# A hybrid decoder block on one core: quarter-array products of a recurrence issued in turns

## The chip, the core and the metric

The kernel runs on one core of one Trainium2 chip. TensorE multiplies matrices in a 128x128 array: a product takes a stationary operand (weights, loaded first) and streams a moving operand through it; results go to PSUM, in which this kernel keeps eight tiles of 128 partitions by 512 fp32 columns. A product whose contraction uses 64 partitions and whose output has 64 partitions occupies one quarter of the array: the half of the rows in which its operands lie, and the half of the columns that belongs to the partitions of its output. The profile prints such a product as 64*64. VectorE (DVE), ScalarE (ACT) and GpSimd (POOL) work elementwise and move PSUM results to SBUF; SyncE (SP) issues most loads from memory. [...]

The metric is the device time of one execution in microseconds (us), the median of several runs. Lower is better.

## The reference

One trunk layer on 512 tokens of 1024 channels: a norm, one wide projection, a sparse attention mixer (compressed, selected and window branches), an RWKV-7 mixer, two gates, an output projection with residual, then a gated MLP with a short convolution. Cut to the parts that the change touches:

```python
def compress_blocks(kv, pe, w1, w2):          # blocks of 32 tokens, stride 16 -> 31 compressed keys or values
    ...
    return jax.nn.gelu(flat @ w1) @ w2        # w2 is the second layer, 256 -> 64

def step(state, inp):                         # RWKV-7: 8 heads, state 64x64 per head, 512 tokens
    r_t, w_t, k_t, v_t, a_t, b_t = inp
    sa = jnp.einsum('bhij,bhj->bhi', state, a_t)
    state = state * w_t[:, :, None, :] + sa[..., None] * b_t[:, :, None, :] + v_t[..., None] * k_t[:, :, None, :]
    return state, jnp.einsum('bhij,bhj->bhi', state, r_t)
_, y = lax.scan(step, state0, xs)             # then a norm per head, a bonus term and a gate
```

## The kernel before

The dense projections keep fp32 accuracy with split operands: activations and weights are cut into a high and a low part, and three products (high x high, low x high, high x low) are summed. Weights arrive as `raw` tiles through SP (three buffers); ACT writes the high part `whi` and DVE or, for a few tiles, POOL the low part `wlo` (two buffers each, line 306).

The recurrence (lines 976 to 1032) is computed in eight chunks of 64 tokens. Products of the eight heads are laid out in four pairs `p` of two heads `r`; head `r` lives on partitions 64r to 64r+63. For chunk `c`, in the order in which TensorE gets it:

1. products from the carried state `M0` into `X` (operand `AR[...,0]`) and then into the output `Y` (operand `AR[...,1]`), 8 products each; both write partitions 64r, so both use the same two quarters. In the profile they are `ps_b<-M,AR` and `ps_a<-M,AR`.
2. DVE copies `X` to `Xs`; meanwhile TensorE runs a piece of other work ("fill").
3. 8 products of the inverse with `Xs` into `U` (`ps_b<-Xs,AB`), then 8 products `x_own` that begin the next chunk's `X` (`ps_b<-UV,AB`). The first use the quarters (rows r, columns r), the second (rows 1-r, columns r).
4. ACT and DVE copy `U` into `UV`; a piece of fill runs meanwhile.
5. 8 products for the next state (`ps_a<-UV,BKT`), which DVE turns into `M`, and 8 more that complete `Y` (`ps_a<-UV,AB`); ACT copies `Y` to `Ys`. Another piece of fill follows.

The fill is a generator, `fill_chain` (line 922): the rest of the keys' and values' projection, `compress`, and the gates' projections. In this stage TensorE's order is written by hand (`manual_schedule` with TensorE alone); the other engines' order comes from a scheduler.

`compress` (line 828) ends with the second layer: a group of 4 small products for the keys and 4 pairs for the values, and after each pair of the values an ACT copy into `vcb`, all from one PSUM bank `kc_ps`.

Ahead of the recurrence, the triangular inverses are put together from 32x32 blocks (`below`, `left`, lines 782 to 800): two visits of `below`, two of `left`, with pieces of a projection of width 280 (`kv_proj(1, 280)`) between them. That projection has three weight tiles; POOL writes all three low parts, and the third takes the buffer of the first.

Of the kernel before, what the change touches and what calls it, by code (L numbers as in the profile page):

```python
# [23 lines left out]
DH = 64  # L24
H = 8
NH2 = H // 2
C = 64
NCH = S // C
# [55 lines left out]
def hybrid_block(ctx: ExitStack, tc: tile.TileContext, A: dict, out: bass.AP):  # L84
# [34 lines left out]
    def pb():  # L119
        return bank("b", 2)  # L120

    def mm(o, l, r, start, stop):
        te.matmul(o, lhsT=l, rhs=r, start=start, stop=stop)  # L123

    def act(o, i, f=AF.Copy, **kw):
        sc.activation(o, i, f, **kw)  # L126
# [278 lines left out]
    def run(g):  # L405
        while True:
            try:
                next(g)
            except StopIteration as e:
                return e.value  # L410
# [23 lines left out]
    AR = mp.tile([128, NH2, NCH, 2, C], F32, name="AR", tag="AR")  # L434

    AB = abp.tile([128, NCH, NH2, 2, 128], F32, name="AB")
    BKT = rp.tile([128, NCH, NH2, 2, DH], F32, name="BKT")
    UV = rp.tile([128, NCH, NH2, 2, DH], F32, name="UV")
# [227 lines left out]
    for g in range(2):  # L666
        for b in range(2):
            r = 64 * g + 32 * b
# [107 lines left out]
    for b in (1, 0):  # L776
        for g in range(2):
            r = 64 * g + 32 * b
# [14 lines left out]
    def left(q0):  # L793
        ptr = [pa(), pb()]
        for i in range(16):
            for g in range(2):
                mm(ptr[g][half(g, 0), 32 * i:32 * i + 32], Y1[half(g, 1), q0 + i], ABq[g][half(g, 1), q0 + i, 32:64],
                   True, True)
        for g in range(2):
            act(ABq[g][half(g, 0), q0:q0 + 16, 32:64], ptr[g][half(g, 0)].rearrange("p (q t) -> p q t", t=32))  # L800
# [3 lines left out]
    with tc.manual_schedule(engines={mybir.EngineType.PE, mybir.EngineType.Pool}):  # L804
        for m in range(NGA):
            act(siga[m], dense_fm(hh, hl))
        below(0)
        below(16)
        next(fill)
        left(0)  # L810
        next(fill)
        left(16)
        next(fill)
        norm_keys(0)
        rstd(qss.rearrange("p t h -> p (t h)"), DH)
        for t in range(NT):
            nc.gpsimd.tensor_tensor(heads(qn[:, t]), heads(qn[:, t]), qss[:, t, :, None].to_broadcast([128, 8, DH]),
                                    op=ALU.mult)
# [11 lines left out]
    def compress():  # L830
        Rk = [sg1[:, 2 * a:2 * a + 2].rearrange("p m s -> p (m s)").rearrange("p (j g n) -> p j g n", j=16, g=2)
              for a in range(2)]
        for a, s_ in enumerate("kv"):
            v.memset(Rk[a][:, :, :, 31:32], 0.0)
            r0 = ROWS["cmp_pe_" + s_][0]
            for g in range(2):
                dv = Dc[:, a, g].rearrange("p (n j) -> p j n", j=8)
                for jh in range(2):
                    tt(Rk[a][:, 8 * jh:8 * jh + 8, g, 0:31], dv[:, :, jh:31 + jh],
                       prm[:, r0 + 8 * jh:r0 + 8 * jh + 8, None].to_broadcast([128, 8, 31]), ALU.add)  # L840
        cw2, hid, hidT, kcd = (QK[:, o:o + 256] for o in range(3072, 4096, 256))
        cw2 = cw2.rearrange("p (a m d) -> p a m d", a=2, m=2)
        hidT = hidT.rearrange("p (m a n) -> p m a n", m=2, a=2)
        kcd = kcd[0:32].rearrange("p (g a d) -> p g a d", g=2, a=2)
        kcs = cp.tile([32, 2], F32, name="kcs")
        yield
        hx = mmb()[:, 0:256]
        for s4 in range(4):
            w = [wnext(4, 256) for _ in range(2)]
            for j in range(4):  # L850
                for a in range(2):
                    mm(hx[64 * a:64 * a + 64], Rk[a][:, 4 * s4 + j].rearrange("p g n -> p (g n)"), w[a][:, j],
                       s4 + j == 0, s4 + j == 6)
            if s4 == 1:
                for a, s_ in enumerate("kv"):
                    nc.sync.dma_start(cw2[:, a], A["cmp_w2_" + s_][0].rearrange("(m p) d -> p m d", p=128))
            yield
        act(hid, hx, AF.Square)
        ts(hid, hid, 0.044715, 1.0)
        tt(hid, hid, hx, ALU.mult)  # L860
        act(hid, hid, AF.Tanh, scale=math.sqrt(2.0 / math.pi))
        stt(hid, hid, 1.0, hx, ALU.add, ALU.mult)
        yield
        pt = mmb()
        for m in range(2):
            te.transpose(pt[:, 128 * m:128 * m + 128], hid[:, 128 * m:128 * m + 128], ident)
        act(hidT.rearrange("p m a n -> p (m a n)"), pt[:, 0:256])
        yield
        kc_ps = mmb()
        for g in range(2):  # L870
            for m in range(2):
                mm(kc_ps[0:32, 64 * g:64 * g + 64], hidT[:, m, 0, 32 * g:32 * g + 32], cw2[:, 0, m], m == 0, m == 1)
        nc.gpsimd.memset(vcb, 0.0)
        for g in range(2):
            for e in range(2):
                bs = slice(64 * g + 32 * e, 64 * g + 32 * e + 32)
                for m in range(2):
                    mm(kc_ps[bs, 128:192], hidT[:, m, 1, 32 * g:32 * g + 32], cw2[:, 1, m], m == 0, m == 1)
                act(vcb[bs, 2 * g + e], kc_ps[bs, 128:192], AF.Copy, scale=0.5)
        for g in range(2):  # L880
            act(kcd[:, g, 0], kc_ps[0:32, 64 * g:64 * g + 64], AF.Copy, scale=0.5)
            act(kcd[:, g, 1], kcd[:, g, 0], AF.Square, accum_out=kcs[:, g:g + 1])
        rstd(kcs, DH)
        for g in range(2):
            ts(kcd[:, g, 1], kcd[:, g, 0], kcs[:, g:g + 1], None)
            ts(kcd[:, g, 0], kcd[:, g, 0], kcs[:, g:g + 1], None)
        yield
        pt = mmb()
        for g in range(2):
            te.transpose(pt[:, 32 * g:32 * g + 32], kcd[:, g].rearrange("p a d -> p (a d)"), ident[0:32, 0:32])  # L890
        ptv = pt[:, 0:64].rearrange("p (g n) -> p g n", g=2)
        act(KC[:, :, 0], ptv, AF.Copy, scale=kg)
        stt(KC[:, :, 1], ptv, kg, KC[:, :, 0].bitcast(F32), ALU.mult, ALU.subtract)

    def group_norm(c0, Ys):
# [6 lines left out]
        act(sq, Ys, AF.Square)  # L902
        v.tensor_reduce(n1, sq, axis=AX.X, op=ALU.add)
        rstd(n1, DH, 64e-5, "g")
# [55 lines left out]
    def hsl(r, n=64):  # L960
        return slice(64 * r, 64 * r + n)

    def x_own(c, X):
        for p in range(NH2):
            for r in range(2):
                o = hsl(1 - r)
                mm(X[hsl(r), 64 * p:64 * p + 64], AB[o, c, p, r, 0:64], UV[o, c, p, r, :], p == 0,
                   c == 0 and p == NH2 - 1)


    with tc.manual_schedule(engines={mybir.EngineType.PE}):
        M0 = Ys = gn = None
        X = pb()
        x_own(0, X)
        next(fill, None)
        for c in range(NCH):
            Y = pa()
            if M0 is not None:
                for p in range(NH2):
                    for r in range(2):  # L980
                        mm(X[hsl(r), 64 * p:64 * p + 64], AR[hsl(r), p, c, 0, :], M0[hsl(r), p, :], False,
                           p == NH2 - 1)
                for p in range(NH2):
                    for r in range(2):
                        mm(Y[hsl(r), 64 * p:64 * p + 64], AR[hsl(r), p, c, 1, :], M0[hsl(r), p, :], p == 0, False)
            Xs = tp.tile([128, NH2, DH], F32, name="Xs", tag="Xs", bufs=2)
            v.tensor_copy(Xs, X[:, 0:256].rearrange("p (a d) -> p a d", d=DH))
            next(fill, None)
            U = pb()
            for p in range(NH2):  # L990
                for r in range(2):
                    mm(U[hsl(r), 64 * p:64 * p + 64], AB[hsl(r), c, p, r, 0:64], Xs[hsl(r), p], True, True)
            act(UV[0:64, c, :, 0, :], U[0:64, 0:256].rearrange("p (a d) -> p a d", d=DH))
            v.tensor_copy(UV[64:128, c, :, 1, :], U[64:128, 0:256].rearrange("p (a d) -> p a d", d=DH))
            if c < NCH - 1:
                X = pb()
                x_own(c + 1, X)
            next(fill, None)
            if c < NCH - 1:
                Mp = pa()  # L1000
# [10 lines left out]
                    tt(M1, M1, pc, ALU.mult)  # L1011
            for p in range(NH2):
                for r in range(2):
                    mm(Y[hsl(r), 64 * p:64 * p + 64], AB[:, c, p, r, 64:128], UV[:, c, p, r, :],
                       M0 is None and p == 0, p == NH2 - 1)
            if c % 2 == 0:
                Ys = tp.tile([128, H, DH], F32, name="Ys", tag="Ys", bufs=2)
            for r in range(2):
                act(Ys[hsl(c % 2), r::2, :], Y[hsl(r), 0:256].rearrange("p (h d) -> p h d", d=DH))
            if c % 2 == 1:  # L1020
                gn = group_norm(c - 1, Ys)
                if c < NCH - 1:
# [1 line left out]
            M0 = M1  # L1024
# [306 lines left out]
    with tc.manual_schedule(engines=KTS):  # L1331
        for t in range(NT):
            qs = slice(128 * t, 128 * t + 128)
            p = mmb()
# [66 lines left out]
    for f in range(NF):  # L1401
# [4 lines left out]
        g = f // 2  # L1406
# [222 lines left out]
```

## Time and profile before

| | |
|---|---|
| median of 3 runs | 834.87 us (834.24 to 835.76) |
| profiled execution | 834.91 us, its span 833.1 us |
| TensorE busy | 812.8 us, 98% of the span |
| DVE, ACT, POOL busy | 604.0, 440.7, 70.5 us |
| stretch 165 to 290 us (inverses' end, recurrence) | TensorE busy 123.97 of 125.00 us |
| granted TensorE clock | full in every slice |

The span is what lies between the first and the last instruction; 1.8 us of the profiled execution lie outside it. A row of the timeline gives the start, the time until the last of its instructions ends, the engine, the line, what is written from what, the shape and the count. A product of fp32 operands stands as two instructions, one for each pass, so that 8 products are a row of x16. Line 123 is the helper through which all products go, so the tiles' names tell them apart. A busy TensorE is a sequence of overlapping instructions: a start-to-start distance says more than a duration.

### The profile page before, as it was taken

To read this page: it belongs to the slowest core of one execution; us is meant where nothing else is said; L and a number is where in the kernel's file an instruction comes from. 1 tells how busy PE (TensorE), PEld (TensorE's weight loads), DVE (VectorE), ACT (ScalarE), POOL (GpSimd) and SP (SyncE) were. 2 spreads that over 40 slices of the span, in tenths; PEclk is the share of its full clock that TensorE was granted. 3 is DMA by queue.
4 is the path that set the end of the run, shared out by engine and by line. 5 is a ranking of instruction groups with operands and counts; after the bars stand their busy time and mean duration, and the time that the engine had idled before them with its cause. 6 is when DMAs were issued, how large, how long until landed. Compare 5 with 4: busy or idle time off the path is not lost.

```text
span 833.1 us, 13078 instructions
## 1 busy us (share of the span) xinstructions
PE 812.8 (98%) x5039; PEld 663.3 (80%) x5039; DVE 604.0 (72%) x1154; ACT 440.7 (53%) x847; POOL 70.5 (8%) x92
## 2 busy tenths in 40 slices
PE   7999999999999999999999999999999999999997
PEld 5788878897778886787788888888888888877886
DVE  5678889963655578888585467667666677769997
ACT  6777755452545677776444354444444444453452
POOL 5200020140000020011000000000000000002101
PEclk9999999999999999999999999999999999999999
DMA  7432322335452230000147143333333332375753
GB/s 217 117 101 71 82 64 77 93 105 159 127 114 65 64 89 13 14 27 26 51 161 254 40 154 99 101 101 100 90 91 100 101 101 86 122 272 183 231 190 142
DMA packets 111394, 91.59 MB, mean 110 GB/s; under 512 B 4237, under 2 KB 98116, under 8 KB 111204
## 3 DMA queue, kind: packets, MB, share of 16 engines
q1 hardware_dynamic: 106192, 75.34, 30.9%
q0 software_dynamic: 4080, 12.87, 4.9%
q10 hardware_dynamic: 1060, 2.55, 1.0%
q8 instruction: 39, 0.64, 0.3%
q14 instruction: 23, 0.19, 0.1%
HBM read 85.30 MB, written 4.39 MB: 108 GB/s over the span
## 4 chain that ended last, share of the span: by engine, by line
PE 49%; DVE 2%; ACT 1%; DMA 1%; issue 0%; DVEq 0%; ACTq 0%
PE ps_mm L123 42%; PE ps_b L123 3%; PE ps_a L123 3%; DMA raw<-in_w_down_dram 1%; DVE wlo L306 1%; ACT whi L126 1%; DVE hl L138 0%; DVE raw L129 0%; DVE a L129 0%; DVE x1b L1437 0%; PE ps_b L1227 0%; ACT a L126 0%; PE ps_a L203 0%; PE ps_mm L1227 0%; ACT hh L126 0%
## 5 line engine op out<-in xcount | busy, mean ns | idle before, releaser
L123 PE MATMUL ps_mm<-hh,whi 128*128 128x512 f32 (+1 forms) x624 | 242.5, 390 | 0.4 <-ACT hh L126 0.3
L123 PE MATMUL ps_mm<-hl,whi 128*128 128x512 f32 (+1 forms) x624 | 238.9, 385 | 0.3 <-DVE hl L138 0.2
L306 DVE TENSOR_TENSOR wlo<-raw,whi 128x1024 fp32r<-128x1024 f32 (+1 forms) x107 | 125.5, 1174 | 95.8 <-PE ps_mm L123 74.4
L126 ACT ACTIVATE whi<-raw 128x1024 fp32r<-128x1024 f32 (+2 forms) x130 | 128.3, 988 | 100.9 <-PE ps_mm L123 42.5
L123 PE MATMUL ps_mm<-hh,wlo 128*128 128x512 f32 (+1 forms) x624 | 151.8, 384 | 0.0
L123 PEld LDWEIGHTS ps_mm<-hh,whi 128*128 128x128 f32 x624 | 117.2, 188 | 26.0 <-issue 1.1
L123 PEld LDWEIGHTS ps_mm<-hl,whi 128*128 128x128 f32 x624 | 117.3, 188 | 23.4 <-DVE hl L138 1.0
L123 PEld LDWEIGHTS ps_mm<-hh,wlo 128*128 128x128 f32 x624 | 115.1, 188 | 23.4
L138 DVE SCALAR_TENSOR_TENSOR cgq<-ps_mm,cw,cgq 128x511 f32<-128x511 f32 (+1 forms) x88 | 65.4, 746 | 1.6
L126 ACT ACTIVATE cgq<-ps_mm,cw 128x512 f32<-128x512 f32 x44 | 34.4, 781 | 19.5 <-PE ps_mm L123 18.9
L126 ACT ACTIVATE P<-P,nm 128x512 f32<-128x512 f32 (+3 forms) x64 | 35.4, 553 | 14.9 <-DVE nm L1201 14.9
L126 ACT ACTIVATE a<-cgq 128x512 fp32r<-128x512 f32 (+2 forms) x24 | 13.2, 549 | 54.1 <-DVE cgq L129 54.1
L129 DVE TENSOR_TENSOR cgq<-cgq 128x512 f32<-128x512 f32 (+1 forms) x52 | 36.4, 700 | 3.6 <-DMA cgq<-in_w_down_dram 1.9
L126 ACT ACTIVATE cgq<-cgq 128x512 f32<-128x512 f32 x22 | 13.9, 632 | 45.0 <-DVE cgq L138 45.0
L306 POOL TENSOR_TENSOR wlo<-raw,whi 128x512 fp32r<-128x512 f32 (+3 forms) x13 | 20.4, 1572 | 146.3 <-PE ps_mm L123 57.3
L1201 DVE CUSTOM_DVE_ANT_0 P<-ps_a,AB 128x512 f32<-128x512 f32 (+3 forms) x64 | 29.4, 483 | 4.2 <-PE ps_a L123 3.7
L1460 POOL DMA_DIRECT2D cgq<-in_w_down_dram x12 | 6.4, 535 | 296.6 <-DVE cgq L129 246.7
L126 ACT ACTIVATE ring<-cgq 128x1024 fp32r<-128x1024 f32 x12 | 12.7, 1062 | 19.4 <-PE ps_b L123 12.1
L123 PE MATMUL ps_a<-KH,qst 128*128 128x512 f32 (+3 forms) x64 | 21.3, 348 | 1.6 <-DVE nm L1201 0.9
L123 PE MATMUL ps_mm<-whi,hh 128*128 128x280 f32 (+2 forms) x72 | 22.4, 333 | 0.4 <-DVE AB L129 0.4
L126 ACT ACTIVATE QK<-ps_mm 128x64 f32<-128x64 f32 (+5 forms) x56 | 14.8, 307 | 14.4 <-PE ps_mm L123 14.3
L123 PE MATMUL ps_mm<-whi,hl 128*128 128x280 f32 (+2 forms) x72 | 21.7, 323 | 0.0
(427 smaller groups left out, 1486.1 us busy)
## 6 DMA issues: line engine op xcount, KB each, us to landing
raw<-in_w_up_dram SPq DMA_DIRECT2D x44, 512.0 KB, 3.8
raw<-in_w_in_dram SPq DMA_DIRECT2D x38, 512.0 KB, 3.9
raw<-in_w_down_dram SPq DMA_DIRECT2D x25, 512.0 KB, 4.5
cgq<-in_w_down_dram POOLq DMA_DIRECT2D x12, 512.0 KB, 4.6
raw<-in_w_out_dram SPq DMA_DIRECT2D x8, 512.0 KB, 3.6
xt<-in_x_dram SPq DMA_DIRECT2D x4, 512.0 KB, 5.8
raw<-in_cmp_w_k_dram SPq DMA_DIRECT2D x4, 512.0 KB, 4.2
raw<-in_cmp_w_v_dram SPq DMA_DIRECT2D x4, 512.0 KB, 4.8
```

The source lines that it names most:

```text
L123: te.matmul(o, lhsT=l, rhs=r, start=start, stop=stop)
L126: sc.activation(o, i, f, **kw)
L129: v.tensor_tensor(o, a, b, op=op)
L138: v.scalar_tensor_tensor(o, a, s, b, op0=op0, op1=op1)
L306: eng.tensor_tensor(lo, raw, hi.bitcast(F32), op=ALU.subtract)
L1201: v.tensor_tensor_reduce(out=P[:, i], in0=sp[:, N * (i - i0):N * (i - i0) + N], in1=BT[:, h, 384 - 128 * qt:512], scale=-1.0, scalar=-NEG, ...
L1460: nc.gpsimd.dma_start(raws[g][i], A["w_down"][0][256 * g + 128 * i:256 * g + 128 * i + 128])
```

## The change

- In step 1, the products into `X` and into `Y` are issued in turns, one of each. The `Y` products now write the partitions of the other head (`hsl(1 - r)`), so they use the quarters (rows r, columns 1-r), which `X` does not use. The products that complete `Y` and the copies to `Ys` are exchanged in the same way.
- In step 3, the products into `U` and the `x_own` products of the next chunk are issued in turns. The copies of `U` stand behind both.
- In `compress`, all products of the second layer come first and the four ACT copies behind them.
- `left(16)` follows `left(0)` directly; the piece of fill that stood between them comes after.

```diff
@@ the inverses @@
         left(0)
+        left(16)
         next(fill)
-        left(16)
         next(fill)
@@ compress @@
                     mm(kc_ps[bs, 128:192], hidT[:, m, 1, 32 * g:32 * g + 32], cw2[:, 1, m], m == 0, m == 1)
+        for g in range(2):
+            for e in range(2):
+                bs = slice(64 * g + 32 * e, 64 * g + 32 * e + 32)
                 act(vcb[bs, 2 * g + e], kc_ps[bs, 128:192], AF.Copy, scale=0.5)
@@ the recurrence @@
+    def in_turns(*gens):
+        gens = list(gens)
+        while gens:
+            for g in list(gens):
+                if next(g, gens) is gens:
+                    gens.remove(g)
+
+    def from_state(c, a, B, off, start, stop):
+        for p in range(NH2):
+            for r in range(2):
+                mm(B[hsl(1 - r if off else r), 64 * p:64 * p + 64], AR[hsl(r), p, c, a, :], M0[hsl(r), p, :],
+                   start and p == 0, stop and p == NH2 - 1)
+                yield
+
+    def through(c, U, Xs):
+        for p in range(NH2):
+            for r in range(2):
+                mm(U[hsl(r), 64 * p:64 * p + 64], AB[hsl(r), c, p, r, 0:64], Xs[hsl(r), p], True, True)
+                yield
...
-                for p in range(NH2):
-                    for r in range(2):
-                        mm(X[hsl(r), 64 * p:64 * p + 64], AR[hsl(r), p, c, 0, :], M0[hsl(r), p, :], False,
-                           p == NH2 - 1)
-                for p in range(NH2):
-                    for r in range(2):
-                        mm(Y[hsl(r), 64 * p:64 * p + 64], AR[hsl(r), p, c, 1, :], M0[hsl(r), p, :], p == 0, False)
+                in_turns(from_state(c, 0, X, False, False, True), from_state(c, 1, Y, True, True, False))
...
-            for p in range(NH2):
-                for r in range(2):
-                    mm(U[hsl(r), 64 * p:64 * p + 64], AB[hsl(r), c, p, r, 0:64], Xs[hsl(r), p], True, True)
+            if c < NCH - 1:
+                X = pb()
+                in_turns(through(c, U, Xs), x_own(c + 1, X))
+            else:
+                run(through(c, U, Xs))
             act(UV[0:64, c, :, 0, :], U[0:64, 0:256].rearrange("p (a d) -> p a d", d=DH))
             v.tensor_copy(UV[64:128, c, :, 1, :], U[64:128, 0:256].rearrange("p (a d) -> p a d", d=DH))
-            if c < NCH - 1:
-                X = pb()
-                x_own(c + 1, X)
...
-                    mm(Y[hsl(r), 64 * p:64 * p + 64], AB[:, c, p, r, 64:128], UV[:, c, p, r, :],
+                    mm(Y[hsl(1 - r), 64 * p:64 * p + 64], AB[:, c, p, r, 64:128], UV[:, c, p, r, :],
...
-                act(Ys[hsl(c % 2), r::2, :], Y[hsl(r), 0:256].rearrange("p (h d) -> p h d", d=DH))
+                act(Ys[hsl(c % 2), r::2, :], Y[hsl(1 - r), 0:256].rearrange("p (h d) -> p h d", d=DH))
```

How TensorE's order changes is shown at three places.

TensorE, recurrence, chunk 1, the products from the state (`M` is the carried state, `AR` the rows of `X` and `Y`, `ps_b` is `X`, `ps_a` is `Y`); before:

```order
L123 MATMUL ps_mm<-hl,whi 128x512
L123 MATMUL ps_b<-M,AR 64x64 [waits DVE_49]
L123 MATMUL ps_b<-M,AR 64x64 x7
L123 MATMUL ps_a<-M,AR 64x64 [waits PE_49]
L123 MATMUL ps_a<-M,AR 64x64 x7
L123 MATMUL ps_mm<-hh,whi 128x512
```

and now:

```order
L123 MATMUL ps_mm<-hl,whi 128x512
L123 MATMUL ps_b<-M,AR 64x64 [waits DVE_49]
L123 MATMUL ps_a<-M,AR 64x64 [waits PE_49]
L123 MATMUL ps_b<-M,AR 64x64
L123 MATMUL ps_a<-M,AR 64x64
...
L123 MATMUL ps_mm<-hh,whi 128x512
```

The 16 products are the same; `Y`'s first has moved from the ninth place to the second, with its wait. The products of `U` and `x_own` are mixed in the same way.

TensorE, second layer of the compression (`QK` holds its operands), chunk 4; before:

```order
L123 MATMUL ps_mm<-QK 32x64 [waits Activation_49]
L123 MATMUL ps_mm<-QK 32x64 x5
L123 MATMUL ps_mm<-QK 32x64 [waits Activation_49]
L123 MATMUL ps_mm<-QK 32x64
...
L123 MATMUL ps_mm<-hh,whi 128x512
```

and now:

```order
L123 MATMUL ps_mm<-QK 32x64 [waits Activation_49]
L123 MATMUL ps_mm<-QK 32x64 x11
L123 MATMUL ps_mm<-hh,whi 128x512
L123 MATMUL ps_mm<-hl,whi 128x512
L123 MATMUL ps_mm<-hh,whi 128x512
```

Three waits for ACT have gone from between the products.

TensorE, the second visit of `left` (`AB` holds the blocks, `sg` the inverses), a piece of the difference. The `wlo` rows between are the fill's 12 products with the first tile's low part:

```order
+L123 MATMUL ps_a<-AB,sg_1239 32x32
+L123 MATMUL ps_b<-AB,sg_1239 32x32
 L123 MATMUL ps_mm<-wlo,hh 128x280 x12
-L123 MATMUL ps_a<-AB,sg_1239 32x32
-L123 MATMUL ps_b<-AB,sg_1239 32x32
 L123 MATMUL ps_mm<-whi,hh 128x280
 L123 MATMUL ps_mm<-whi,hl 128x280
```

The 32 small products (two of them shown) stood between the 12 products with `wlo` and the next 10 with `whi`; now these follow each other.

More of the change, by code (lines that the diff above doesn't have):

```diff
@@ L968, in x_own @@
                    c == 0 and p == NH2 - 1)
+                yield
[15 more added lines that the diff above has]
+                mm(U[hsl(r), 64 * p:64 * p + 64], AB[hsl(r), c, p, r, 0:64], Xs[hsl(r), p], True, True)
+                yield
     with tc.manual_schedule(engines={mybir.EngineType.PE}):
@@ L973, in hybrid_block @@
         X = pb()
-        x_own(0, X)
+        run(x_own(0, X))
         next(fill, None)
```

## The prediction

> **What bounds the kernel now.** I read the page first, then a view of the stage by windows, then who waits for whom there, then the timeline of TensorE around each edit.
>
> ```profile
> PE 812.8 (98%) x5039; PEld 663.3 (80%) x5039; DVE 604.0 (72%) x1154; ACT 440.7 (53%) x847; POOL 70.5 (8%) x92
> PEclk9999999999999999999999999999999999999999
> 165.00:290.00 125.00, 123.97 (x1486) 99.98 (x1484) 69.34 (x171) 60.84 (x135) 11.59 (x15) 1.00 0.42 107
> 290.00:410.00 120.00, 116.71 (x771) 91.31 (x770) 95.42 (x309) 83.83 (x217) 14.30 (x16) 1.00 0.14 36
> PE ps_mm L123 <- ACT kc L126: 0.9, 3, 0.3
> DVE Xs L987 <- PE ps_b L123: 12.5, 4, 4.0
> DVE M L129 <- PE ps_a L123: 11.1, 4, 3.4
> ```
>
> The first two rows are from the page, the next two are stretches by windows (length, then busy time of PE, PEld, DVE, ACT, POOL), and the last three are waits around this stage (us, count, the longest). From 165 to 290 us TensorE is busy for 123.97 of 125 us at the full clock, and the only wait that the trace names for it is 0.9 us, for the ACT copies of the compression. DVE waits for TensorE, not the reverse. So TensorE's own time is the path here, and a microsecond that its instructions need less should reach the end; all four edits lie in this stretch. From 290 to 410 us it is idle for 120 - 116.71 = 3.3 us, in chains with ACT and DVE that begin from its own products and so move with it as a whole.
>
> **The recurrence's products.** The timeline of TensorE in chunk 1 (start, us until the last ends, what, count of passes):
>
> ```profile
> 193.84 0.68 PE L123 MATMUL ps_b<-M,AR 64*64 64x64 f32 x16
> 194.36 0.63 PE L123 MATMUL ps_a<-M,AR 64*64 64x64 f32 x16
> 194.92 0.50 PE L123 MATMUL ps_mm<-hh,whi 128*128 128x512 f32 x1
> ...
> 197.87 0.51 PE L123 MATMUL ps_b<-Xs,AB 64*64 64x64 f32 x10
> 198.16 0.27 PE L123 MATMUL ps_b<-UV,AB 64*64 64x64 f32 x2
> 198.21 0.28 PE L123 MATMUL ps_b<-Xs,AB 64*64 64x64 f32 x3
> 198.27 0.22 PE L123 MATMUL ps_b<-UV,AB 64*64 64x64 f32 x1
> 198.28 0.22 PE L123 MATMUL ps_b<-Xs,AB 64*64 64x64 f32 x1
> 198.28 0.22 PE L123 MATMUL ps_b<-UV,AB 64*64 64x64 f32 x1
> 198.33 0.22 PE L123 MATMUL ps_b<-Xs,AB 64*64 64x64 f32 x1
> 198.33 0.22 PE L123 MATMUL ps_b<-UV,AB 64*64 64x64 f32 x1
> 198.33 0.22 PE L123 MATMUL ps_b<-Xs,AB 64*64 64x64 f32 x1
> 198.34 0.51 PE L123 MATMUL ps_b<-UV,AB 64*64 64x64 f32 x11
> 198.78 0.44 PE L123 MATMUL ps_mm<-raw,sg 128*64 128x256 f32 x2
> ```
>
> The two groups from the state take 194.92 - 193.84 = 1.08 us, one after the other, on the same two quarters. `U` and `x_own` take 198.78 - 197.87 = 0.91 us for as many passes, and the rows say why: they lie on different quarters, and for a moment all four run. From 198.21 to 198.34, 0.13 us, eight passes start, four of `Xs` and four of `UV`, two per quarter: a quarter starts a pass every 0.06 us. In the last row `UV` is alone on two quarters: the 11th pass ends at 198.85 and takes 0.22, so it started at 198.63, ten starts after 198.34, five per quarter: 0.29 / 5 = 0.058. A quarter keeps its pace whether two run or four. That is the row that carries the forecast: what `in_turns` makes the rule has happened by chance here for a tenth of a microsecond.
>
> A group of 16 products now gives each quarter 8 passes. The first row of `Xs` has ten starts, five per quarter, the last at 197.87 + 0.51 - 0.22 = 198.16, so four distances of a quarter fill 0.29 us; at 0.058 for three of them the first is 0.11. From the last start to the first of other work it is 198.78 - 198.63 = 0.15. So 0.11 + 6 x 0.058 + 0.15, with 0.02 for four quarters begun one behind the other: 0.63 us. If the first loads of four quarters get in each other's way, as they never do in this trace, I allow 0.70. From below, no less than this is to be had while a quarter needs 0.058.
>
> From the state, chunks 1 to 7: 7 x (1.08 - 0.63) = 3.15 us less. `U` with `x_own`, chunks 0 to 6: 0.28 each. `X` and `U` are complete no later than before, since each needs the same 0.46 us from its first start to its last; but what came behind them on TensorE, and covered the copies, is gone. One place has no cover to give:
>
> ```profile
> 217.40 1.07 PE L123 MATMUL ps_a<-UV,BKT 128*64 128x64 f32 x15
> ...
> 246.12 0.69 PE L123 MATMUL ps_a<-UV,BKT 128*64 128x64 f32 x16
> ...
> 214.68 1.06 ACT L126 ACTIVATE whi<-raw 128x1024 fp32r<-128x1024 f32 x1 [3.13 <-DMA raw<-in_w_in_dram]
> ...
> 215.77 1.23 DVE L306 TENSOR_TENSOR wlo<-raw,whi 128x1024 fp32r<-128x1024 f32 x1 [0.89 <-ACT whi L126]
> 217.36 0.43 DVE L994 COPY UV<-ps_b 64x256 f32<-64x256 f32 x1
> ```
>
> In chunk 2 the state's products need 1.07 us against 0.69 for 16 passes in chunk 4, since DVE's `UV` copy ends only at 217.79; it stands behind a `wlo`, which waited for `whi`, which waited for a load. ACT had been idle for that load since 211.55, before `U` began, so the copy does not come sooner for a shorter `U`: chunk 2 gives its 0.28 back as a longer wait. Six chunks are left: 6 x 0.28 = 1.7 us; with chunk 2, 2.0 at most. The tightest of the others is chunk 4, where the chain of the compression stands ahead of the copy:
>
> ```profile
> 240.51 0.16 DVE L135 TENSOR_SCALAR rs_m<-kcs 32x2 f32<-32x2 f32 x1 [1.00 <-ACT QK L126]
> ...
> 243.78 0.43 DVE L994 COPY UV<-ps_b 64x256 f32<-64x256 f32 x1
> ```
>
> There 246.12 - 244.21 = 1.9 us lie between copy and use. The edit in the compression takes 1.8 of them from TensorE's side and `U` 0.28, but DVE's chain, which today waits 1.00 us for ACT, begins about 1 us sooner too. I expect no wait; 0.5 us if I am wrong. The exchanged heads move nothing between engines. Where the products into the state end on one pair of columns and those into `Y` now begin on the same, a quarter may wait a pass or two, up to 0.05 in each of 8 chunks; I take 0.1 together, 0 to 0.4.
>
> **The compression's second layer.**
>
> ```profile
> 236.38 0.86 PE L123 MATMUL ps_mm<-QK 128*32 128x64 f32 x12
> 237.54 0.41 PE L123 MATMUL ps_mm<-QK 128*32 128x64 f32 x4 [0.30 <-ACT kc L126]
> ...
> 238.97 0.41 PE L123 MATMUL ps_mm<-QK 128*32 128x64 f32 x4 [0.30 <-ACT kc L126]
> 239.31 0.50 PE L123 MATMUL ps_mm<-hh,whi 128*128 128x512 f32 x1
> ```
>
> It takes 239.31 - 236.38 = 2.93 us. Twelve passes alone start within 0.86 - 0.22 = 0.64, 0.058 each, on one strip of 32 columns. If all 24 go one behind the other: 23 x 0.058 + 0.15 = 1.5 us, a gain of 1.4. But the last 12 passes lie on three other strips of columns, and strips have just been seen to run side by side: then 12 passes, four more and the tail, about 1.1 us. I take the nearer case to the rows above: 1.8 us less (1.4 to 1.9). ACT's four copies stand behind all of them, and the next step that needs them is three pieces of fill away.
>
> **One left visit.**
>
> ```profile
> 171.90 0.28 PE L123 MATMUL ps_mm<-whi,hl 128*128 128x280 f32 x1
> 172.11 0.21 PE L123 MATMUL ps_a<-AB,sg 32*32 32x32 f32 x1
> ...
> 173.24 0.40 PE L123 MATMUL ps_mm<-wlo,hh 128*128 128x280 f32 x1
> ...
> 174.37 0.67 PE L123 MATMUL ps_mm<-wlo,hh 128*128 128x280 f32 x4
> ...
> 176.10 0.40 PE L123 MATMUL ps_mm<-whi,hh 128*128 128x280 f32 x1
> 176.34 0.29 PE L123 MATMUL ps_mm<-whi,hl 128*128 128x280 f32 x1
> ...
> 177.50 0.81 PE L123 MATMUL ps_mm<-wlo,hh 128*128 128x280 f32 x5
> ...
> 175.52 1.42 POOL L306 TENSOR_TENSOR wlo<-raw,whi 128x560 fp32r<-128x560 f32 x1 [6.67 <-ACT AB L126]
> ```
>
> The projection's products follow each other at (0.67 - 0.29) / 3 = 0.13, by the row of x4. Coming into a visit costs 172.11 - 171.90 = 0.21 instead, coming out 176.34 - 176.10 = 0.24 instead, and the tail of the last small product about 0.1 more, by the groups above: 0.3 us per visit, of which one goes. But something is late next. POOL's third `wlo` takes the first one's buffer, which TensorE leaves when the row of 174.37 ends, at 175.04; POOL starts 0.47 later and needs 1.42. TensorE asks for it at the fourth of the five products of 177.50, at 177.89, 0.9 us after it is there. Now the second visit stands ahead and takes 173.24 - 172.11 - 0.12 = 1.0 us: the first `wlo` is left at 176.05, while TensorE, without a visit between, asks 14 steps of 0.13 after its last start of 175.76, at 177.58. POOL ends at 177.6 to 177.95, by whether it needs 0.1 or 0.47 to begin; with the signal TensorE waits 0.1 to 0.4. I take 0.3: this edit is worth nothing, between 0.3 gained and 0.2 lost.
>
> **The sum.** 3.15 + 1.7 + 1.8 + 0 - 0.1 = 6.55 us, made against the profiled execution's 834.91 (834.9 - 6.5 = 828.4), which stands 0.04 above the median of the runs, so the median should be **828.3 us**. Its own range: everything at its best is 3.15 + 2.0 + 1.9 + 0.3 = 7.35, to 827.5; groups of 0.70, 1.4 for the compression, 0.2 lost at the visit and 0.4 for the exchange give 7 x 0.38 + 6 x 0.21 + 1.4 - 0.6 = 4.7, to 830.2.
>
> **Rivals.** First, the copies do not keep up. If `UV`, `Xs` or `M` come late in half of the chunks, about half of the recurrence's 4.85 us is waited away again: 831 to 831.5 us. For it speaks chunk 2; against it the rows in which DVE waits for TensorE.
>
> Second, the quarters do not do what the change wants: those that share rows take turns. Then both kinds of groups stay at 1.08 and 0.91, and only the compression is left: 834.9 - 1.8 + 0.1, 833.2 us, which cannot be told from no change. Against it stand the eight starts in 0.13 us. [...]
>
> Third, starts have a floor: TensorE begins a pass every 0.029 us, the pace of the last `UV` row, on however many quarters. A group of 32 then needs 32 x 0.029 + 0.15 = 1.08: nothing less from the state, 7 x 0.17 more at `U`, and with the compression 834.9 + 1.2 - 1.8 + 0.1 = 834.4 us, no change. Against it, eight starts in 0.13 us are 0.016 each. [...]
>
> Fourth, slower: alternating between two quarters of the same rows uncovers the loading of weights. Then each pass costs a half of the rows 0.11, the distance of a quarter's first two starts, instead of 0.058 for two quarters at once: 16 x 0.11 + 0.15 = 1.9 us per group, 7 x 0.8 + 7 x 1.0 = 12.6 more and 1.7 less, 845.8 us. It decides as soon as a half of the rows needs over 0.058 us a pass, since then the groups gain nothing. It needs a conflict in steady state that the mixed rows do not show.
>
> **How the numbers follow.** The forecast 78%, late copies 10%, taking turns 5%, the floor 3%, uncovered loads 4%. What a measurement of this kernel can tell from no change is 0.2%, 1.7 us. Faster are the first two of these: 0.88; within 0.2% the next two, 0.08; slower the last, 0.04. The forecast's 827.5 to 830.2 would hold some two thirds; reaching to late copies, and a little below, 827.0 to 831.5 holds 8 in 10.
>
> **What would show it.** Right: `ps_b<-M,AR` and `ps_a<-M,AR` mixed in the timeline, 0.63 us from the first to the next dense product, and the same for `Xs` and `UV`; no row in which TensorE waits for `UV` but chunk 2, longer by 0.3 than now; the second layer in one run of 1.1 to 1.5 us; and behind the left visit a wait of `ps_mm` for POOL of 0.1 to 0.4. Wrong: groups of 0.9 or more (turns or the floor), of 1.5 or more (uncovered loads), or new waits for DVE in several chunks.

## The result and the profile after

The changed kernel takes 829.0 us (828.42 to 830.58) beside 835.32 for the kernel before: a ratio of 0.9932, with a 95% interval of 0.9919 to 0.9944. That is faster by 5.7 us of 834.9, between 4.7 and 6.8. Measured once more, with six runs, it took 828.01 beside 834.28, a ratio of 0.9926 (0.9913 to 0.9938). The profiled execution took 829.55 us.

The page, and the waits of TensorE around the stretch (us in total, times, the longest):

```profile
span 827.8 us, 13078 instructions
PE 807.3 (98%) x5039; PEld 658.5 (80%) x5039; DVE 603.2 (73%) x1154; ACT 440.5 (53%) x847; POOL 70.1 (8%) x92
```

```profile
PE ps_a L123 <- DVE UV L1013: 1.1, 1, 1.1
PE ps_mm L123 <- POOL wlo L306: 0.6, 1, 0.6
PE ps_a L123 <- ACT UV L126: 0.2, 1, 0.2
```

TensorE is busy for 812.8 - 807.3 = 5.5 us less. The three waits for ACT's `kc` have gone, and three others stand there that before did not name: two in chunk 2, one at the left visit.

The products from the state in chunk 1, and the second layer, in the timeline of TensorE:

```profile
193.72 0.27 PE L123 MATMUL ps_b<-M,AR 64*64 64x64 f32 x1
193.73 0.27 PE L123 MATMUL ps_a<-M,AR 64*64 64x64 f32 x1
193.73 0.27 PE L123 MATMUL ps_b<-M,AR 64*64 64x64 f32 x1
193.74 0.27 PE L123 MATMUL ps_a<-M,AR 64*64 64x64 f32 x1
193.83 0.22 PE L123 MATMUL ps_b<-M,AR 64*64 64x64 f32 x1
...
193.89 0.22 PE L123 MATMUL ps_b<-M,AR 64*64 64x64 f32 x1
...
194.35 0.50 PE L123 MATMUL ps_mm<-hh,whi 128*128 128x512 f32 x1
...
234.90 0.92 PE L123 MATMUL ps_mm<-QK 128*32 128x64 f32 x24
235.74 0.50 PE L123 MATMUL ps_mm<-hh,whi 128*128 128x512 f32 x1
```

The first passes of the four quarters start within 0.02 us. Each quarter starts its second pass 0.11 us after its first, and then one every 0.058. From the first start to the next dense product it is 194.35 - 193.72 = 0.63 us, against 1.08 before, in all seven chunks. `U` with `x_own` takes 0.63 as well, against 0.91. The second layer takes 235.74 - 234.90 = 0.84 us, against 2.93, in one run.

The left visit, in the timelines of TensorE, POOL and DVE:

```profile
176.80 0.55 PE L123 MATMUL ps_mm<-wlo,hh 128*128 128x280 f32 x3
177.94 0.53 PE L123 MATMUL ps_mm<-wlo,hh 128*128 128x280 f32 x2 [0.60 <-POOL wlo L306]
178.40 0.27 PE L123 MATMUL ps_b<-UV,AB 64*64 64x64 f32 x2
...
176.15 1.73 POOL L306 TENSOR_TENSOR wlo<-raw,whi 128x560 fp32r<-128x560 f32 x1 [7.69 <-ACT AB L126]
...
176.62 2.25 DVE L129 TENSOR_TENSOR sg<-QK,prm 128x248 f32<-128x248 f32 x2
```

By the 0.13 from product to product TensorE asks for POOL's low part 0.39 us behind 176.80, at 177.19; it goes on at 177.94, 0.75 us later. POOL's operation ends at 176.15 + 1.73 = 177.88.

Chunk 2 in the timeline of TensorE, which waits there first for ACT's half of `UV` and then for DVE's; the first two rows are the kernel before, the others the changed one:

```profile
215.47 2.00 PE L123 MATMUL ps_mm<-hh,wlo 128*128 128x512 f32 x8
...
218.92 0.50 PE L123 MATMUL ps_mm<-hh,whi 128*128 128x512 f32 x1
```

```profile
216.10 0.33 PE L123 MATMUL ps_a<-UV,BKT 128*64 128x64 f32 x2 [0.19 <-ACT UV L126]
217.58 0.62 PE L123 MATMUL ps_a<-UV,BKT 128*64 128x64 f32 x13 [1.15 <-DVE UV L1013]
...
218.65 0.50 PE L123 MATMUL ps_mm<-hh,whi 128*128 128x512 f32 x1
```

The first dense product behind the inverses' `below` starts at 168.82 in the kernel before and at 168.43 in the changed one. TensorE begins its last work ahead of `UV`, eight products with `wlo`, at 215.47 and at 213.92: 46.65 and 45.49 us behind that start, so 1.16 sooner in the changed kernel. But the dense product behind the group starts 50.10 us behind it before and 50.22 now. What was saved up to here is waited away here.

What that copy waits for, followed back through SP's loads, ACT's `whi` and DVE's `wlo` (timelines of the three engines):

```profile
183.57 0.46 SPq L277 DMA_DIRECT2D raw<-in_w_in_dram  x1
...
188.73 1.06 ACT L126 ACTIVATE whi<-raw 128x1024 fp32r<-128x1024 f32 x1 [1.84 <-PE ps_a L123]
...
189.82 1.23 DVE L306 TENSOR_TENSOR wlo<-raw,whi 128x1024 fp32r<-128x1024 f32 x1 [0.73 <-ACT whi L126]
...
191.07 0.37 SPq L277 DMA_DIRECT2D raw<-in_cmp_w_k_dram  x1
...
198.40 1.06 ACT L126 ACTIVATE whi<-raw 128x1024 fp32r<-128x1024 f32 x1 [6.84 <-DMA raw<-in_w_in_dram]
...
200.75 0.37 SPq L277 DMA_DIRECT2D raw<-in_cmp_w_k_dram  x1
...
208.20 1.06 ACT L126 ACTIVATE whi<-raw 128x1024 fp32r<-128x1024 f32 x1 [3.48 <-DMA raw<-in_w_in_dram]
...
210.54 2.05 SPq L277 DMA_DIRECT2D raw<-in_w_in_dram  x3
...
214.41 1.06 ACT L126 ACTIVATE whi<-raw 128x1024 fp32r<-128x1024 f32 x1 [3.21 <-DMA raw<-in_w_in_dram]
...
217.09 0.43 DVE L1013 COPY UV<-ps_b 64x256 f32<-64x256 f32 x1
```

A `wlo` gives its `raw` back and SP then issues three loads within 1 to 1.8 us. ACT's next `whi` waits for one of them (the last of the three in the first two rounds, the first in the third), DVE's `wlo` follows, and so on, from 183.57 to 217.09. The row of 188.73 names a product of TensorE, which ended at 188.61, but it is the load: its landing stands at 188.62, 5.05 us behind its issue. In the kernel before, the same `whi` starts at 188.57 and its row names the load, while these products of TensorE end only at 188.74; and in all profiles it begins 5.1 to 5.2 us behind the issue of the load. So after 183.57 nothing that TensorE does stands in this chain. It sets the pace of chunks 0 to 2. Its start does move with TensorE: in all profiles the load of 183.57 is issued 5.2 us behind the first `x_own` product, whether that stands at 9.1 or at 10.0 us behind `below`.

### The profile page after: what moved, and what is told of

It is laid out like the page before. It is cut to its first block, busy times and chain, and to the rows that moved or that the text cites. A ratio compares the mean times of both kernels' runs of the same rounds, so it can differ in the third digit from the quotient of the medians.

```text
span 827.8 us, 13078 instructions
## 1 busy us (share of the span) xinstructions
PE 807.3 (98%) x5039; PEld 658.5 (80%) x5039; DVE 603.2 (73%) x1154; ACT 440.5 (53%) x847; POOL 70.1 (8%) x92
## 3 DMA queue, kind: packets, MB, share of 16 engines
HBM read 85.30 MB, written 4.39 MB: 108 GB/s over the span
## 4 chain that ended last, share of the span: by engine, by line
PE 48%; DVE 3%; DMA 1%; ACT 1%; issue 1%; DVEq 0%; ACTq 0%; POOLq 0%
PE ps_mm L123 41%; PE ps_b L123 3%; PE ps_a L123 3%; DVE wlo L306 1%; DMA cgq<-in_w_down_dram 1%; DVE hl L138 0%; ACT whi L126 0%; DVE raw L129 0%; DVE a L129 0%; DVE x1b L1453 0%; PE ps_b L1243 0%; ACT a L126 0%; PE ps_a L203 0%; PE ps_mm L1243 0%; DVE cgq L138 0%
```

## The experiments

One table holds what all profiles say of the stretch, since single runs differ by 2 us and more. Times count, as above, from the first dense product behind the inverses' `below`, read from each profile's timelines: the end of the last copy of `UV` in chunk 2, the start of the first dense product behind chunk 7's products into `Y`, and the difference.

| kernel | last `UV` copy, chunk 2 | end of chunk 7 | difference |
|---|---|---|---|
| before | 48.97 | 116.30 | 67.33 |
| changed, two profiles | 49.09; 48.93 | 110.88; 110.72 | 61.79; 61.79 |
| state_only | 48.95 | 114.00 | 65.05 |
| own_only | 48.54 | 114.68 | 66.14 |
| layer2_only | 48.41 | 113.77 | 65.36 |
| left_undone | 48.64 | 110.45 | 61.81 |
| left_late | 48.51 | 110.32 | 61.81 |
| exch_no_turns | 49.40 | 112.64 | 63.24 |
| turns_no_exch | 49.29 | 113.66 | 64.37 |
| same_rows | 48.55 | 111.83 | 63.28 |
| uv_act, two profiles | 47.87; 48.10 | 109.66; 109.90 | 61.79; 61.80 |
| left_late_uv_act | 46.92 | 108.71 | 61.79 |

Behind the copy everything is TensorE's own time, to a hundredth: five kernels with the same products have 61.8. Ahead of it stands a time between 48.4 and 49.4 that the loads set, whatever TensorE saved; it is less only where ACT copies both halves (the last two rows).

### One part of the change alone

**state_only**: the kernel before, with

```diff
-                for p in range(NH2): ... mm(X[hsl(r), ...], AR[hsl(r), p, c, 0, :], M0[hsl(r), p, :], ...)
-                for p in range(NH2): ... mm(Y[hsl(r), ...], AR[hsl(r), p, c, 1, :], M0[hsl(r), p, :], ...)
+                in_turns(from_state(c, 0, X, False, False, True), from_state(c, 1, Y, True, True, False))
```

and the exchanged heads in the products and copies of `Y`.

> The kernel before with one part of the change: the products from the state in turns, with Y's heads exchanged. In the changed kernel such a group takes 0.625 us instead of 1.078 in each of 7 chunks. Theory (loads): from 183 us to the UV copy of chunk 2 a chain of weight loads, whi and wlo copies runs by itself, so what TensorE saves in chunks 1 and 2 is waited away there: TensorE's wait for DVE's UV in chunk 2 grows from 0.3 by 0.9 to 1.2 us, and 5 x 0.453 = 2.3 us are left, 832.6 us by a before of 834.9. Rival (each product counts): the wait stays near 0.3, 7 x 0.453 = 3.2 us, 831.7.

Measured: 831.73 us, a ratio of 0.9972 (0.9964 to 0.9981), 2.3 us (1.6 to 3.0). The wait, from the view of waits:

```profile
PE ps_a L123 <- DVE UV L1006: 1.0, 1, 1.0
```

The stretch is 116.30 - 114.00 = 2.30 us shorter, and its copy of `UV` ends at 48.95, where it ended before at 48.97 though two groups ahead of it were 0.453 us shorter each. The theory of the loads holds; the rival's 3.2 does not. The wait is 1.0 where the theory had 1.2.

**own_only**: the kernel before with `in_turns(through(c, U, Xs), x_own(c + 1, X))`, nothing else.

> The kernel before with U's and x_own's products in turns, nothing else. Theory (loads): 0.28 us less in each of chunks 0 to 6, of which chunks 0 to 2 are waited away at chunk 2 (its wait grows from 0.3 to 1.1 us), so that 4 x 0.28 = 1.1 us are left. Rival (each product counts, with chunk 2 alone given back): 1.7 us, chunk 2's wait 0.6.

Measured: 831.99 us, a single run. Behind the copy 67.33 - 66.14 = 1.19 us are gained, as the loads' theory has it. But the wait is 0.5 us, near the rival's 0.6, and the whole stretch gained 1.62, near the rival's 1.7, since the copy came 48.97 - 48.54 = 0.43 sooner. In the other profiles in which DVE makes its half, the copy comes at 48.4 to 49.4, so 0.43 lies within what the loads differ by from run to run; this run alone does not decide between the two.

**layer2_only**: the kernel before, with the four ACT copies behind all products.

> The kernel before with the compression's second layer whole, nothing else. It stands in chunk 4, behind the wait of chunk 2. In the changed kernel the layer took 0.845 us instead of 2.93. Theory: all 2.09 us reach the end, 832.8 us by a before of 834.9, and no wait for the copies of kc turns up later. Rival: the chain of small DVE operations behind the copies comes late at the copy of UV in chunk 4, and 0.3 to 0.5 us of it are waited away there.

Measured: 831.86 us, a ratio of 0.9976 (0.9965 to 0.9988), 2.0 us (1.0 to 2.9). No wait of TensorE is named from 155 to 288 us, not in chunk 4 either. The stretch is 2.53 shorter: 2.09 are the layer (0.845 us instead of 2.932), and the other 0.44 are from chunk 2, where the copy came 0.56 sooner and TensorE had no wait. The rival falls.

**left_undone**: the changed kernel, with

```diff
         left(0)
-        left(16)
         next(fill)
+        left(16)
         next(fill)
```

> The changed kernel with the second left visit put back between the two pieces of fill. Theory (loads, started by the visit): TensorE's wait of 0.6 us for POOL's wlo is gone, the first x_own product comes 0.55 us sooner counted from the inverses' below, and since the loads that end in chunk 2 start from TensorE's products behind it, they come 0.55 sooner too: 0.55 us faster than the changed kernel, 828.4, chunk 2's wait unchanged at 1.1. Rival (loads fixed by something else): chunk 2's wait grows to 1.65 and the time stays at 829.0.

Measured: 828.75 us, a ratio of 0.9941 (0.9927 to 0.9955), which cannot be told from the changed kernel. In the profile POOL's `wlo` took 1.38 us, the wait for it is gone, `x_own` starts 0.55 sooner, and so do the first two rounds of loads. The wait in chunk 2 stays at 1.1, as the theory has it and the rival does not. Of the 0.55, 0.29 to 0.45 are left at the `UV` copy. Over all profiles, the five with two visits end that copy at 48.41 to 48.97, the five with one visit ahead of the low part's products at 48.55 to 49.40: means of 48.70 and 49.05. That is 0.35 us for the visit, with a spread of 0.56 and 0.85 within the two groups; the starts of `x_own` show that it costs and doesn't gain, the size at the end is not settled.

### What makes the quarters run together

**exch_no_turns**: the changed kernel, with

```diff
-                in_turns(from_state(c, 0, X, False, False, True), from_state(c, 1, Y, True, True, False))
+                run(from_state(c, 0, X, False, False, True))
+                run(from_state(c, 1, Y, True, True, False))
```

> The changed kernel, but the products from the state are issued one group after the other again, X's 8 and then Y's 8; Y keeps the exchanged heads, so the two groups lie on different quarters. Theory (TensorE begins a pass early only a few places down its order): the groups overlap for the last passes only, as U and x_own did before, 0.9 us from the first start to the next dense product in each of 7 chunks. Rival (the quarters alone matter, whatever the order): 0.63, as in the changed kernel.

Measured: 830.37 us, a single run, and in the timeline of TensorE, chunk 1:

```profile
194.67 0.51 PE L123 MATMUL ps_b<-M,AR 64*64 64x64 f32 x10
194.97 0.27 PE L123 MATMUL ps_a<-M,AR 64*64 64x64 f32 x2
195.01 0.28 PE L123 MATMUL ps_b<-M,AR 64*64 64x64 f32 x3
...
195.58 0.50 PE L123 MATMUL ps_mm<-hh,whi 128*128 128x512 f32 x1
```

195.58 - 194.67 = 0.91: the first passes of `Y` start when ten of `X` have started and six are still to come, and the overlap is only that. The rival's 0.63 does not come. Other quarters alone bring 0.17 us of the 0.45 per group, the turns the rest.

**turns_no_exch**: the changed kernel, `Y` back on its own heads.

```diff
-    ... from_state(c, 1, Y, True, True, False))
+    ... from_state(c, 1, Y, False, True, False))
```

> The changed kernel with the heads of Y not exchanged: X's and Y's products are still issued in turns, on the same two quarters. Theory (a quarter starts a pass every 0.058 us, whoever it belongs to): 16 passes per quarter, 1.08 us per group as before the change. Rival (alternating between two outputs costs on a quarter): more than 1.1.

Measured: 832.3 us, a single run.

```profile
194.08 0.34 PE L123 MATMUL ps_b<-M,AR 64*64 64x64 f32 x4
194.25 0.29 PE L123 MATMUL ps_a<-M,AR 64*64 64x64 f32 x4
...
195.21 0.50 PE L123 MATMUL ps_mm<-hh,whi 128*128 128x512 f32 x1
```

195.21 - 194.08 = 1.13 us, 0.05 above the group of before and on the rival's side of 1.1. So turns without other quarters are worth nothing and cost a little; where the 0.05 come from was not followed.

**same_rows**: the changed kernel, first the eight passes on each of the two quarters of one half of the rows, then those of the other half.

```diff
-                in_turns(from_state(c, 0, X, False, False, True), from_state(c, 1, Y, True, True, False))
+                for r_ in range(2):
+                    in_turns(from_state(c, 0, X, False, False, True, (r_,)),
+                             from_state(c, 1, Y, True, True, False, (r_,)))
```

> The changed kernel with the products from the state in another order: first those of one half of the rows, X's and Y's in turns, so that only two quarters with the same rows run, then those of the other half. Theory (every quarter keeps its own 0.058 us): the two halves follow each other, 0.9 to 1.1 us per group. Rival (quarters of the same rows load their weights in turns): 16 passes of 0.058 for each half of the rows, 1.9 to 2.0 us per group; with two free halves running side by side that would not have shown in the changed kernel only if each needed no more than half of that.

Measured: 828.86 us, a single run.

```profile
193.69 0.27 PE L123 MATMUL ps_b<-M,AR 64*64 64x64 f32 x1
193.70 0.27 PE L123 MATMUL ps_a<-M,AR 64*64 64x64 f32 x1
193.80 0.22 PE L123 MATMUL ps_b<-M,AR 64*64 64x64 f32 x1
193.81 0.22 PE L123 MATMUL ps_a<-M,AR 64*64 64x64 f32 x1
193.86 0.22 PE L123 MATMUL ps_b<-M,AR 64*64 64x64 f32 x1
...
193.99 0.27 PE L123 MATMUL ps_b<-M,AR 64*64 64x64 f32 x1
...
194.60 0.50 PE L123 MATMUL ps_mm<-hh,whi 128*128 128x512 f32 x1
```

While only quarters of the same rows run, from 193.69 to 193.99, each starts its passes every 0.058 us after the first 0.11, and the group takes 0.91. The rival with 1.9 to 2.0 falls. The two halves overlap from 193.99 on, as in exch_no_turns: ten passes have started, six stand ahead.

### Taking the waits away

**uv_act**, and the same kernel again beside the changed one: in chunk 2 ACT copies both halves of `UV`.

```diff
-            v.tensor_copy(UV[64:128, c, :, 1, :], ...)
+            (act if c == 2 else v.tensor_copy)(UV[64:128, c, :, 1, :], ...)
```

> The changed kernel with one copy moved: in chunk 2 both halves of UV are copied by ACT, instead of one by ACT and one by DVE, where it stands behind a wlo that waits for a load. Theory: TensorE's wait there falls from 1.3 us (1.1 for DVE, 0.2 for ACT) to some 0.3 to 0.5, as ACT ends its second copy at about 216.4 where DVE ended at 217.5; what comes behind finds its weights ready: 0.8 to 1.1 us faster than the changed kernel, 828.0 us. Rival: the fill behind needs the same load's low part or the next load, and the wait moves there: no gain, 829.0.

> The kernel of uv_act once more, beside the changed one. Theory (loads): 109.7 us from below to the last products into Y, as in its first profile, no wait for UV in chunk 2, and 1.2 us below the changed kernel. Rival (the first profile was chance, or what is gained is waited away behind 290 us): the same time as the changed kernel.

The timelines of ACT and TensorE, first profile:

```profile
215.40 0.76 ACT L126 ACTIVATE UV<-ps_b 64x256 f32<-64x256 f32 x2
...
215.81 1.02 PE L123 MATMUL ps_a<-UV,BKT 128*64 128x64 f32 x15
```

The wait in chunk 2 is down to about 0.3 us in the first profile (1.02 us, where 16 such passes take 0.69 without a wait), and the fill behind finds its weights. Between the end of `below` and of chunk 7 the two profiles take 1.2 and 0.8 us less than the changed kernel's. But the time does not show it, as the rival of the second expectation had it: 829.48 us, a ratio of 0.9945 (0.9931 to 0.9959), and then 828.14, 0.9934 (0.9918 to 0.9950), beside 0.9926 for the changed kernel. Some of what was gained is given back at the very end, in all three profiles with this edit and in none of the others. The rows are the issue of the last store and the DMA queue that brings instructions (packets, MB, share), first in the changed kernel (the queue from 822.4 to 823.2 us), then in uv_act (from 823.0 to 824.3 us):

```profile
824.31 0.38 ACTq L1616 DMA_DIRECT2D out_dram<-x1b  x1
```

```profile
q14 instruction: 1, 0.01, 2.4%
```

```profile
821.96 0.38 ACTq L1616 DMA_DIRECT2D out_dram<-x1b  x1
```

```profile
q14 instruction: 1, 0.01, 2.7%
```

The span ends 827.76 - 824.31 = 3.45 us after that issue in the changed kernel, and 3.43 to 3.45 in the ten other profiles without this edit; in the three with it 4.86, 4.41 and 4.39. In the changed kernel a block of instructions is fetched 1.7 us ahead of the last store's issue, in uv_act as long behind it, among the store's packets; these end 1.4 us behind the issue in the eleven profiles and 1.8 to 2.3 behind it in the three. The edit gives ACT one instruction more and DVE one less. The fetch beside the late landing is seen; that it is the cause, and what moved it, was not tried.

**left_late**: the changed kernel, the visits behind the first low part's products.

```diff
         next(fill)
+        next(fill)
         left(0)
         left(16)
         next(fill)
-        next(fill)
```

> The changed kernel with both left visits still in one place, but behind the 12 products of the first low part instead of ahead of them, so that POOL gets that buffer before the visits. Theory: TensorE's wait for POOL's wlo, 0.6 us, is gone and the one change-over saved stays: the first x_own product 9.2 us behind below instead of 9.97 (two visits: 9.41), the loads start as much sooner, 0.7 us faster than the changed kernel. Rival (the copies of the visits' outputs come late for x_own, as they now begin 1.7 us later): a wait for ACT ahead of x_own and no gain.

Timelines of TensorE and POOL:

```profile
176.79 0.81 PE L123 MATMUL ps_mm<-wlo,hh 128*128 128x280 f32 x5
177.52 0.68 PE L123 MATMUL ps_b<-UV,AB 64*64 64x64 f32 x16
...
173.81 1.37 POOL L306 TENSOR_TENSOR wlo<-raw,whi 128x560 fp32r<-128x560 f32 x1 [5.37 <-issue]
```

POOL's low part is there 1.6 us early, and `x_own` starts 9.12 us behind `below` (9.97 in the changed kernel, 9.41 before): one place for both visits is worth 0.29 us, once nothing waits for it. No wait is named ahead of `x_own`, so the rival falls. The end of chunk 7 comes 0.4 to 0.56 sooner, since the loads do, where the theory had 0.7; the time, 828.35 us, ratio 0.9925 (0.9912 to 0.9939), does not show it.

**left_late_uv_act**: both edits.

> Both edits on the changed kernel: the visits behind the first low part's products, and both halves of UV by ACT in chunk 2. Theory (they add): 1.2 + 0.7 = 1.9 us below the changed kernel, no wait of TensorE from 160 to 280 us, 109.0 us from below to the last products into Y. Rival: with the wait for UV gone the loads do not set the time there, the earlier start of the loads is worth nothing by itself, but TensorE's own 0.75 are: the same sum; if instead the fill behind chunk 2 waits for its weights, 0.5 to 1 us less.

Measured: 828.19 us, a ratio of 0.9922 (0.9910 to 0.9934). TensorE has no wait named from 155 to 288 us, and the stretch takes 108.71, 2.0 less than the changed kernel's second profile: the edits add. Yet the median is that of the changed kernel, 828.01. Of the 2.0 the late landing at the end takes 1.0. The rest is inside the spread: from the end of chunk 7 to the issue of the last store the fourteen profiles take 543.1 to 545.8 us, and the stretch begins between 168.3 and 170.0 us. In four of the five profiles whose mean granted clock was 0.997 or 0.998 it began at 169.4 or later (169.98 here), in those with 0.999 or 1.0 by 168.9. A version that beats the changed kernel is not shown.

> The changed kernel itself, beside the next three, since single runs of one kernel here differ by 2 us. Every theory: 5.7 to 6.3 us below the kernel before, and from the end of the inverses' below to the last products into Y 110.9 us as in its profile, within the 0.5 by which the loads of chunk 2 differ.

The changed kernel itself came as expected: 828.01 us and 110.72.

## Why the prediction came out

The time lies 0.7 us above the 828.3 forecast and inside both ranges. Step by step:

- **The row that carried the forecast**: miscounted, without harm. From 198.21 to 198.34 the rows show ten starts, six of `Xs` and four of `UV`, not eight. That is a start every 0.014 us instead of 0.016, and a quarter's 0.058 stands.
- **From state, 3.15**: right. 1.08 to 0.63 in each of seven chunks. The "first loads of four quarters" do not get in each other's way: the first passes start within 0.02 us, and each quarter's second 0.11 behind its first.
- **`U` and `x_own`, 0.28 each**: right in size, 0.906 to 0.625 in seven chunks.
- **Second layer, 1.8**: that all its passes run without a break was right; the size was 2.09, beyond the 1.4 to 1.9 allowed. The 1.1 allowed "12 passes, four more and the tail"; the three other strips begin beside the first strip's last three passes and the layer takes 0.84.
- **Left visit, 0**: wrong by 0.55 at its place. The reason was right and was the one given, POOL's third `wlo`. POOL started 0.48 us after TensorE had left the buffer, the slow case foreseen. The change-over saved is 0.29, as forecast (left_late). The wait was mis-sized: it cost 9.97 - 9.12 = 0.85 where 0.1 to 0.4 was allowed, 0.3 of it because POOL took 1.73 us instead of 1.42, and 0.1 because the two products behind the wait took 178.40 - 177.94 = 0.46 us, where the same two took 0.35 before. POOL's subtraction met DVE's `sg`, of which one piece took 1.66 us instead of 0.64. Before, in left_undone and in left_late POOL met DVE's small operations instead and took 1.42, 1.38 and 1.37, and one of these small operations took 1.35 to 1.41 us there instead of some 0.2 (`kss`, 128x8: 1.35 before, 0.16 in the changed kernel). That the two engines slow each other where they meet is the author's reading of these times; why they would, no run shows. (The list of engines at the start can be read as if POOL moved PSUM results too. In this kernel none of its operations names a PSUM tile; those copies are DVE's and ACT's.)
- **Exchanged heads, -0.1**: they cost nothing. From the first `ps_a<-UV,BKT` to the next dense product it is 1.08 us in chunk 1 and in chunks 3 to 6, as before.
- **"chunk 2 gives its 0.28 back as a longer wait"**: this is the step that failed. The copy's release by a load was seen, and the copy was rightly said not to come sooner; but then all that TensorE saves ahead of it is given back, not only chunk 2's 0.28. Two groups from the state (0.91) and three of `U` (0.84), less the 0.55 of the visit, are 1.2 us; TensorE was there 1.16 sooner, and waited. The copy ended at 48.97 before and at 49.09 after, so ahead of it nothing was gained, where the sum had 1.46. Behind it 67.33 - 61.79 = 5.54 were gained, where the sum had 2.25 + 1.12 + 1.8 - 0.1 = 5.07. Together 5.42 instead of 6.55.

That the forecast came so close is in part luck: what was counted behind the copy of chunk 2, 0.5 too little, and what was counted ahead of it, 1.6 too much, err in opposite ways. And the size itself is known to about 1 us either way: the profiled execution gained 5.36 us, the two ratios stand for 5.7 and 6.2.

Of the rivals, "the copies do not keep up" happened at one place, chunk 2, not in half of the chunks, by a chain of loads and not by the copies' own length. "Quarters that share rows take turns" and "uncovered weight loads" fell with same_rows, where two quarters with the same rows each kept their 0.058 us, and "the floor" with the changed kernel's starts on four quarters, which lay 0.007 us apart at 193.72 to 193.74.

## What to carry to other kernels

In this kernel products on different quarters of the array ran side by side where they stood close in TensorE's order: issuing them in turns turned 1.08 us into 0.63, and neither other quarters alone (0.91) nor turns alone (1.13) did. Before summing such gains, look for the first place behind them where a load sets the time, follow that load back to what released it, and count only what lies behind that place. A wait whose release does not depend on the engine that waits, even one of 1.07 - 0.69 = 0.4 us as in chunk 2 here, says that what this engine saves between the start of that chain and the wait is worth nothing.

## What the runs showed that was not expected

- TensorE did not start all its passes in the order of its instructions: on free quarters it started some early, but not far ahead. In exch_no_turns, in same_rows and for `U` before the change, the second group begins when ten passes of the first have started and six are still to start. The number is not fixed: in the second layer another strip begins when nine passes of the first strip have started and three are still to start.
- A small change in the number of ACT's and DVE's instructions, 600 us earlier, was met by 1.0 to 1.4 us at the last store, 3 profiles of 3, beside a fetch of instructions that had moved behind its issue.
- The third of the loads ahead of chunk 2 is issued 32.9 to 34.1 us behind `below`, and ACT's `whi` begins at 38.9 to 39.9, by run, in the eleven profiles in which DVE makes its half of the copy, while the first of the three is issued at 31.3 to 32.3; this is most of the spread of the `UV` copies in the table.
